# Mixture-of-experts stage of a decoder block: down weights in whole rows, shared PSUM accumulators, scatters in the next block

## The chip, the core and the metric

The kernel runs on one core of one Trainium2 chip; the other cores are idle. The metric is the device time of one execution in microseconds, taken as the median of several runs. One further execution was taken with the hardware profiler; all rows shown come from it.

## What is computed

The reference is one decoder layer for 512 tokens of width 2048, all in float32: a shared RMSNorm with modulation, sparse attention beside gated linear attention, an output projection, then a mixture of experts and a final RMSNorm. The change is in the mixture of experts alone, which has 32 experts in 4 groups of 8. Each token picks its best group and two experts in it:

```
def expert_ffn(args):
    xb, e = args
    return (jax.nn.silu(xb @ w_gate[e]) * (xb @ w_up[e])) @ w_down[e]

y = lax.map(expert_ffn, (x_slots, blk_expert)).reshape(cap, D)
y = y * slot_w[:, None].astype(y.dtype)
y = jnp.zeros((N + 1, D), y.dtype).at[slot_tok].add(y)[:N]
```

`w_gate` and `w_up` are 2048 x 512 for each expert and `w_down` is 512 x 2048, 4 MiB each. So the stage reads 32 x 12 MiB = 402.7 MB of weights once. Its result, times a gate vector g2, is added to the residual stream x.

## The kernel before, in words

Everything up to the routing takes the first half of the time. It ends with `x1`, the residual stream (4 tiles of 128 tokens), with its normalized copy in two parts whose sum keeps float32 precision (`h2h`, `h2l`), and with each token's places and weights for the experts. Then the experts are sorted by their number of tokens, and the stage runs in **blocks** of 128 token slots (`Block`, L1160). The first block has experts 0 and 1 with 64 slots each. Eleven blocks follow (L1365 to L1367): eight with three experts (one of 64 slots and two of 32), and three with two experts of 64 slots, which come third, sixth and ninth of these eleven. So there are twelve blocks, and the last has three experts. A loop for experts with more tokens than slots comes behind and runs only if it is needed.

A block does the following, for the four chunks n of 512 input columns:

- `gather(n, i)` (L1171): two matmuls with the one-hot matrix G bring the rows of token tile i into the slots; after i = 3, ACT copies the sum out as `xe`.
- `turn(n)` (L1181): four transposes on PE and four ACT activations, which also apply the modulation, give `xt`.
- `gate_up(n, which)` (L1192): for each expert of the block one load of 1 MiB of gate (`which` 0) or up (`which` 1) weights, then the products into two PSUM accumulators `pgu`. The source of a load is 512 whole rows of the matrix, four consecutive ones to a partition, which makes 8192 consecutive bytes for each partition (`load_in`, L1142).

After the last chunk ACT and DVE form silu(gate) x up. `weights` (L1207) makes the transposed one-hot matrix `T` and the slot weights `ws`, and `turn_up` (L1218) transposes the activation to `aT`. Then come the down products, in four steps `down(hf, kk)` (L1226): hf is the half of the 2048 output columns, kk the half of the 512 inner rows. A step loads for each expert 256 rows by 1024 columns, 1 MiB, two pieces of 4096 bytes for each partition (`load_down`, L1153). Each half uses two PSUM accumulators `pd`; after its second step DVE, ACT and DVE again weigh each of the two chunks of 512 columns and split it in two parts `yh`, `yl` (L1241 to L1245). `scatter(n, i)` (L1248) multiplies them with `T` (two matmuls into `pss`) and DVE adds the product to token tile i of `x1` (L1253).

PSUM has eight banks, two each for the tags `pst`, `pgu`, `pd` and `pss` (L1106, `pB`). The weights go through a ring of seven tiles of 1 MiB, four of the pool `ring` and three of `lm` (`wtile`, L1125); all loads are issued by SP in the order of the program, and a load waits until PE has released the tile seven loads before it. PE's order is fixed by hand: `then` (L1258) chains each step behind the one before.

`run_block` (L1266) sets this order. Scatters of output chunks 0 and 1 lie in the block's own down stretch, those of chunks 2 and 3 are woven between the gathers of the next block's chunks 1 and 2:

```
for i in range(NT):
    then(blk.gather, n + 1, i)
    if left and i in (0, 2):
        then(prev.scatter, 2 + n, i // 2)
if left:
    then(prev.scatter, 2 + n, 2)
    then(prev.scatter, 2 + n, 3)
...
then(blk.turn, n + 1)
```

`begin_next` (L1369) makes the one-hot matrix of the next block on DVE and its weighted form on POOL. The last block cuts its last chunk in two (`cuts`, L1376).

## Time and profile before

| what | us |
|---|---|
| median of 3 runs | 2143.22 (2139.55 to 2144.33) |
| profiled execution | 2135.08 |
| its span, first to last instruction | 2133.4 |
| PE busy in it | 1934.6 (91%) |
| DVE busy | 947.4 (44%) |
| ACT busy | 677.0 (32%) |

The profile is of the one execution named. PE is the tensor engine's matmuls and PEld its weight loads, which overlap them; a busy PE is not PE at its peak, since matmuls are pipelined. The DMA share is the mean busy share of the 16 DMA engines, and PEclk the clock granted to PE as a share of 2.4 GHz. A row of the windows gives the stretch, its length, the busy us (and instructions) of PE, PEld, DVE, ACT and POOL, then PEclk, the DMA share and GB/s. A float32 product stands as two matmul rows. An arrow names who ended an idle time.

### The profile page before, as it was taken

Reading aid. Unit: us, or ns where it says so; the run is one execution under the profiler, and the core shown is the slowest. Engines: PE = TensorE matmul, PEld = TensorE weight load, DVE = VectorE, ACT = ScalarE, POOL = GpSimd, SP = SyncE. Lnnn points to the kernel's source line nnn. Section 1 sums busy time; section 2 is a strip of 40 time slices with the busy share of each in tenths; the row PEclk is TensorE's granted clock in tenths of the full one; section 3 lists DMA queues with packets and bytes.
Section 4 is the critical chain, followed back from the end, with each engine's and each line's share of the span. In section 5 each row is a group of like instructions: output and inputs, shape, how many; then the busy total and the mean of one; then the engine's idle time right before and its main releaser. Section 6 shows DMA issues by size and latency. Waiting matters only on the chain. (4 is left out here: it accounts for less than half of the span.)

```text
span 2133.4 us, 29142 instructions
## 1 busy us (share of the span) xinstructions
PE 1934.6 (91%) x11126; PEld 1129.4 (53%) x11126; DVE 947.4 (44%) x2098; ACT 677.0 (32%) x1443; POOL 57.5 (3%) x112
## 2 busy tenths in 40 slices
PE   6989999999999999999979888997889888998885
PEld 4646777777777787877734332442324323343322
DVE  4667876468764965576352121230212311221205
ACT  4433567466543443323342101111112111111112
POOL 0001000000000000100000000000000000000000
PEclk8999999999999999999989999999999999999998
DMA  8996735326463774676248999999999999999995
GB/s 289 315 296 168 207 107 130 88 63 182 122 183 95 219 207 133 222 268 220 99 186 334 413 403 405 397 401 406 413 394 376 419 404 415 397 390 408 394 414 184
DMA packets 241891, 595.42 MB, mean 279 GB/s; under 512 B 23154, under 2 KB 105272, under 8 KB 208724
## 3 DMA queue, kind: packets, MB, share of 16 engines
q1 hardware_dynamic: 227424, 583.05, 74.1%
q10 hardware_dynamic: 11764, 6.27, 1.1%
q0 software_dynamic: 2560, 4.20, 1.0%
q8 instruction: 89, 1.46, 0.3%
q14 instruction: 54, 0.44, 0.1%
HBM read 580.37 MB, written 7.86 MB: 276 GB/s over the span
## 5 line engine op out<-in xcount | busy, mean ns | idle before, releaser
L1199 PE MATMUL pgu<-raw,xt 128*32 128x512 f32 (+1 forms) x2544 | 404.4, 606 | 64.4 <-DMA raw<-in_w_expert_gate_dram 45.2
L1199 PEld LDWEIGHTS pgu<-raw,xt 128*32 128x32 f32 (+1 forms) x2544 | 110.2, 116 | 323.5 <-issue 199.3
L1234 PE MATMUL pd<-raw,aT 128*32 128x512 f32 (+1 forms) x1280 | 246.4, 598 | 31.8 <-DMA raw<-in_w_expert_down_dram 22.1
L360 PE MATMUL pj<-hthi,wlo 128*128 128x512 f32 (+1 forms) x624 | 250.6, 402 | 4.0 <-DVE wlo L355 3.9
L358 PE MATMUL pj<-hthi,whi 128*128 128x512 f32 (+1 forms) x624 | 251.4, 403 | 0.7 <-ACT a L403 0.7
L359 PE MATMUL pj<-htlo,whi 128*128 128x512 f32 (+1 forms) x624 | 249.6, 400 | 0.5 <-issue 0.5
L1253 DVE TENSOR_TENSOR x<-x,pss 128x512 f32<-128x512 f32 (+1 forms) x196 | 127.1, 674 | 257.8 <-PE pss L1252 257.6
L163 DVE SCALAR_TENSOR_TENSOR acc<-raw,csil,acc 128x512 f32<-128x512 f32 x296 | 222.1, 751 | 27.9 <-DMA raw<-in_w_ada_dram 23.5
L1234 PEld LDWEIGHTS pd<-raw,aT 128*32 128x32 f32 (+1 forms) x1280 | 69.8, 114 | 193.3 <-issue 104.0
L1178 ACT COPY xe<-pst 128x512 f32<-128x512 f32 x48 | 28.1, 585 | 391.8 <-PE pst L1175 391.8
L354 ACT CAST whi<-raw 128x512 fp32r<-128x512 f32 (+1 forms) x156 | 94.9, 614 | 177.0 <-PE pj L359 162.4
L355 DVE TENSOR_TENSOR wlo<-raw,whi 128x512 fp32r<-128x512 f32 (+1 forms) x156 | 105.4, 681 | 88.0 <-ACT whi L354 81.9
L360 PEld LDWEIGHTS pj<-hthi,wlo 128*128 128x128 f32 (+1 forms) x624 | 116.6, 187 | 29.9 <-DVE wlo L355 5.2
L358 PEld LDWEIGHTS pj<-hthi,whi 128*128 128x128 f32 (+1 forms) x624 | 116.7, 187 | 26.5 <-issue 3.6
L359 PEld LDWEIGHTS pj<-htlo,whi 128*128 128x128 f32 (+1 forms) x624 | 116.6, 187 | 26.0 <-issue 4.4
L1243 ACT CAST y<-y 128x512 fp32r<-128x512 f32 (+1 forms) x49 | 29.8, 609 | 295.0 <-DVE y L1241 291.6
L1241 DVE SCALAR_TENSOR_TENSOR y<-pd,ws,g2b 128x512 f32<-128x512 f32 (+1 forms) x49 | 36.1, 737 | 170.8 <-PE pd L1234 170.7
L1251 PE MATMUL pss<-y,T 128*128 128x512 f32 (+1 forms) x196 | 87.4, 446 | 14.7 <-DVE x L1253 14.2
L1188 ACT ACTIVATE xt<-pst,modp,w2p 128x128 f32<-128x128 f32 x192 | 73.5, 457 | 37.6 <-PE pst L1185 37.6
L1174 PE MATMUL pst<-h2h,G 128*128 128x512 f32 x192 | 80.9, 421 | 1.4 <-DVE G L1028 1.2
L606 ACT ACTIVATE s<-s,mx 128x128 f32<-128x128 f32 (+3 forms) x128 | 70.9, 556 | 18.5 <-DVE mx L604 17.9
L1252 PE MATMUL pss<-y,T 128*128 128x512 f32 (+1 forms) x196 | 76.6, 391 | 0.0
(479 smaller groups left out, 2668.8 us busy)
## 6 DMA issues: line engine op xcount, KB each, us to landing
raw<-in_w_expert_down_dram SPq DMA_DIRECT2D x128, 1024.0 KB, 11.8
raw<-in_w_expert_gate_dram SPq DMA_DIRECT2D x127, 1024.0 KB, 11.5
raw<-in_w_expert_up_dram SPq DMA_DIRECT2D x127, 1024.0 KB, 10.1
raw<-in_w_ada_dram SPq DMA_DIRECT2D x96, 1024.0 KB, 6.7
raw<-in_w_in_dram SPq DMA_DIRECT2D x38, 1024.0 KB, 6.1
raw<-in_w_out_dram SPq DMA_DIRECT2D x16, 1024.0 KB, 5.2
raw<-in_x_dram SPq DMA_DIRECT2D x8, 1024.0 KB, 6.2
rkv<-in_w_in_dram SPq DMA_DIRECT2D x4, 1024.0 KB, 9.1
```

What stands on the lines that cost most here:

```text
L163: nc.vector.scalar_tensor_tensor(acc, wt[:, k], csil[:, kt:kt + 1], acc, op0=OP.mult, op1=OP.add)
L354: nc.scalar.copy(hi[:, :, 0:n], src)
L355: nc.vector.tensor_sub(lo[:, :, 0:n], src, hi[:, :, 0:n].bitcast(F32))
L358: nc.tensor.matmul(ps[:n], hi[:, k, 0:n], hthi[kt // 4][:, kt % 4], start=(kt == 0), stop=False)
L359: nc.tensor.matmul(ps[:n], hi[:, k, 0:n], htlo[kt // 4][:, kt % 4], start=False, stop=False)
L360: nc.tensor.matmul(ps[:n], lo[:, k, 0:n], hthi[kt // 4][:, kt % 4], start=False, stop=(kt == KT - 1))
L1174: nc.tensor.matmul(self.pg, self.G[:, i], h2h[n][:, i], start=(i == 0), stop=False)
L1199: ins = nc.tensor.matmul(self.gu[which][s0:s0 + u], self.xt[n][:, k, s0:s0 + u], wts[x][k], start=(n == 0 and k == 0), stop=(n == 3 and k ...
L1234: ins = nc.tensor.matmul(self.pd[c][s0:s0 + u], self.aT[:, 2 * kk + k, s0:s0 + u], wts[x][:, k, 512 * c:512 * c + 512], start=(kk == 0 and ...
L1251: nc.tensor.matmul(ps, self.T[:, 128 * i:128 * i + 128], yh, start=True, stop=False)
L1252: ins = nc.tensor.matmul(ps, self.T[:, 128 * i:128 * i + 128], yl, start=False, stop=True)
L1253: nc.vector.tensor_add(x1[:, i, c0:c0 + cn], x1[:, i, c0:c0 + cn], ps)
```

## The change

Down weights are loaded in another cut: step k of four takes for each expert rows 128k to 128k + 127 of `w_down` whole, so each partition gets one row of 8192 consecutive bytes (`load_rows`); the number and size of loads stay. A step multiplies into all four output chunks, so four accumulators are open at once (`down_rows`); gate, up and down share four PSUM banks under one tag `acc` in place of two times two. The weighing becomes a method `weigh(n)`: chunks 0 and 1 are weighed after the down products, chunks 2 and 3 in the next block's chunks 0 and 1. All four scatters move into the next block, one output chunk in each of its four input chunks, between `turn` and the up products; the gathers of a chunk now stand ahead of its gate products, except in the first block. The last block keeps the old down steps and its two own scatters.

```diff
--- before.py
+++ after.py
@@ -1106,7 +1106,7 @@
     psB = LM.enter_context(tc.tile_pool(name="psB", bufs=2, space=PSUM))
 
     def pB(tag):
-        return psB.tile([128, 512], F32, name=tag, tag=tag)
+        return psB.tile([128, 512], F32, name=tag, tag=tag, bufs=4 if tag == "acc" else 2)
 
     g2b = []
 
@@ -1149,6 +1149,12 @@
             return t
         nc.sync.dma_start(t, src)
         return [t[:, k] for k in range(4)]
+
+    def load_rows(e, k):
+
+        t = wtile().rearrange("p k f -> p (k f)")
+        nc.sync.dma_start(t, one(wd_, e)[:, 128 * k:128 * k + 128].rearrange("o p c -> p (o c)"))
+        return t
 
     def load_down(e, kk, hf):
 
@@ -1191,7 +1197,7 @@
 
         def gate_up(self, n, which):
             if n == 0 and which == 0:
-                self.gu = pB("pgu"), pB("pgu")
+                self.gu = pB("acc"), pB("acc")
             wts = [load_in((wg_, wu_)[which], e, n) for e, _, _ in self.experts]
             u = self.unit
             for k in range(4):
@@ -1223,27 +1229,44 @@
             nc.scalar.copy(self.aT, ps.rearrange("p (j s) -> p j s", j=4))
             return ins
 
+        def down_rows(self, k):
+
+            if k == 0:
+                self.pd = [pB("acc") for _ in range(4)]
+            wts = [load_rows(e, k) for e, _, _ in self.experts]
+            u = self.unit
+            for n in range(4):
+                for x, s0 in self.parts:
+                    ins = nc.tensor.matmul(self.pd[n][s0:s0 + u], self.aT[:, k, s0:s0 + u],
+                                           wts[x][:, 512 * n:512 * n + 512], start=(k == 0), stop=(k == 3))
+            return ins
+
         def down(self, hf, kk):
+
             if kk == 0:
-                self.pd = pB("pd"), pB("pd")
+                if hf == 0:
+                    self.pd = [None] * 4
+                self.pd[2 * hf:2 * hf + 2] = pB("acc"), pB("acc")
             wts = [load_down(e, kk, hf) for e, _, _ in self.experts]
             u = self.unit
             for c in range(2):
                 for k in range(2):
                     for x, s0 in self.parts:
-                        ins = nc.tensor.matmul(self.pd[c][s0:s0 + u], self.aT[:, 2 * kk + k, s0:s0 + u],
+                        ins = nc.tensor.matmul(self.pd[2 * hf + c][s0:s0 + u], self.aT[:, 2 * kk + k, s0:s0 + u],
                                                wts[x][:, k, 512 * c:512 * c + 512], start=(kk == 0 and k == 0),
                                                stop=(kk == 1 and k == 1))
                 if kk == 1:
-                    n = 2 * hf + c
-                    for c0, cn in self.cuts if n == 3 else ((0, 512),):
-                        ys, yh, yl = (mp.tile([128, 512], dt, name="y", tag="yz", bufs=5)[:, 0:cn] for dt in (F32, F32R, F32R))
-                        nc.vector.scalar_tensor_tensor(ys, self.pd[c][:, c0:c0 + cn], self.ws, g2b[n][:, c0:c0 + cn],
-                                                       op0=OP.mult, op1=OP.mult)
-                        nc.scalar.copy(yh, ys)
-                        nc.vector.tensor_sub(yl, ys, yh.bitcast(F32))
-                        self.y.setdefault(n, []).append((512 * n + c0, cn, yh, yl))
+                    self.weigh(2 * hf + c)
             return ins
+
+        def weigh(self, n):
+            for c0, cn in self.cuts if n == 3 else ((0, 512),):
+                ys, yh, yl = (mp.tile([128, 512], dt, name="y", tag="yz", bufs=5)[:, 0:cn] for dt in (F32, F32R, F32R))
+                nc.vector.scalar_tensor_tensor(ys, self.pd[n][:, c0:c0 + cn], self.ws, g2b[n][:, c0:c0 + cn],
+                                               op0=OP.mult, op1=OP.mult)
+                nc.scalar.copy(yh, ys)
+                nc.vector.tensor_sub(yl, ys, yh.bitcast(F32))
+                self.y.setdefault(n, []).append((512 * n + c0, cn, yh, yl))
 
         def scatter(self, n, i):
             for c0, cn, yh, yl in self.y[n]:
@@ -1266,21 +1289,28 @@
     def run_block(blk, prev, begin_next):
 
 
+        last = len(blk.cuts) > 1
+
+        def gather(n):
+            before_gather(blk, n)
+            for i in range(NT):
+                then(blk.gather, n, i)
+
         for n in range(4):
+            if n < 3 and blk is not first:
+                gather(n + 1)
             then(blk.gate_up, n, 0)
             if n < 3:
-                before_gather(blk, n + 1)
-                left = prev is not None and n < 2
+                if blk is first:
+                    gather(n + 1)
+                then(blk.turn, n + 1)
+            if prev is not None:
                 for i in range(NT):
-                    then(blk.gather, n + 1, i)
-                    if left and i in (0, 2):
-                        then(prev.scatter, 2 + n, i // 2)
-                if left:
-                    then(prev.scatter, 2 + n, 2)
-                    then(prev.scatter, 2 + n, 3)
-                elif n == 2:
-                    then(blk.weights)
-                then(blk.turn, n + 1)
+                    then(prev.scatter, n, i)
+                if n < 2:
+                    prev.weigh(n + 2)
+            if n == 3:
+                then(blk.weights)
             then(blk.gate_up, n, 1)
         nxt = begin_next()
         if not g2b:
@@ -1291,14 +1321,20 @@
         then(blk.turn_up)
         if nxt is not None:
             then(nxt.turn, 0)
-        then(blk.down, 0, 0)
-        then(blk.down, 0, 1)
-        then(blk.down, 1, 0)
-        for i in range(NT):
-            then(blk.scatter, 0, i)
-        then(blk.down, 1, 1)
-        for i in range(NT):
-            then(blk.scatter, 1, i)
+        if last:
+            then(blk.down, 0, 0)
+            then(blk.down, 0, 1)
+            then(blk.down, 1, 0)
+            for i in range(NT):
+                then(blk.scatter, 0, i)
+            then(blk.down, 1, 1)
+            for i in range(NT):
+                then(blk.scatter, 1, i)
+        else:
+            for k in range(4):
+                then(blk.down_rows, k)
+            blk.weigh(0)
+            blk.weigh(1)
         return nxt
 
 
@@ -1464,7 +1500,7 @@
     rsqrt_small(ssf, ssf, (128, NT), 1.0 / D)
     nfb = []
     for n in range(4):
-        ps = pB(("pst", "pd")[n % 2])
+        ps = pB(("pst", "acc")[n % 2])
         for j in range(4):
             nc.tensor.transpose(ps[:, 128 * j:128 * j + 128],
                                 colv[:, 48 + 4 * n + j:49 + 4 * n + j].to_broadcast([128, 128]), ident)
```

## Rows read from the trace of the kernel before

**Rows 1.** Page, section 2: GB/s in 40 slices, DMA packets.
```profile
GB/s 289 315 296 168 207 107 130 88 63 182 122 183 95 219 207 133 222 268 220 99 186 334 413 403 405 397 401 406 413 394 376 419 404 415 397 390 408 394 414 184
DMA packets 241891, 595.42 MB, mean 279 GB/s; under 512 B 23154, under 2 KB 105272, under 8 KB 208724
```

**Rows 2.** Windows, gate and up stretches: busy us by engine, PEclk, DMA share, GB/s.
```profile
1170.00:1210.00 40.00, 35.27 (x230) 14.91 (x222) 6.62 (x10) 6.84 (x17) 1.29 (x2) 1.00 1.01 418
1262.00:1302.00 40.00, 35.29 (x223) 14.99 (x222) 7.54 (x11) 6.96 (x17) 1.22 (x1) 1.00 1.01 417
1418.00:1458.00 40.00, 36.14 (x244) 15.32 (x236) 7.23 (x12) 6.84 (x17) 1.29 (x2) 1.00 1.01 417
1512.00:1552.00 40.00, 34.64 (x221) 14.58 (x221) 6.68 (x11) 6.84 (x17) 1.20 (x1) 1.00 1.01 413
1672.00:1712.00 40.00, 35.24 (x226) 14.98 (x222) 6.62 (x10) 6.84 (x17) 1.28 (x2) 1.00 1.01 418
1764.00:1804.00 40.00, 35.37 (x222) 14.95 (x222) 6.69 (x11) 6.84 (x17) 1.20 (x1) 1.00 1.01 414
1920.00:1960.00 40.00, 36.79 (x252) 15.70 (x244) 7.39 (x12) 7.16 (x18) 1.20 (x2) 1.00 1.00 408
```

**Rows 3.** Windows, down stretches of the same blocks.
```profile
1225.00:1245.00 20.00, 16.76 (x92) 3.91 (x90) 2.80 (x4) 2.72 (x6) 0.00 (x0) 1.00 1.02 381
1318.00:1338.00 20.00, 16.41 (x98) 4.87 (x98) 2.80 (x4) 2.99 (x7) 0.00 (x0) 1.00 1.02 390
1475.00:1495.00 20.00, 16.49 (x97) 4.84 (x96) 2.79 (x4) 2.90 (x7) 0.00 (x0) 1.00 1.02 389
1568.00:1588.00 20.00, 15.88 (x85) 4.07 (x88) 2.80 (x4) 3.56 (x8) 0.00 (x0) 1.00 1.01 382
1727.00:1747.00 20.00, 16.36 (x97) 5.03 (x98) 2.80 (x4) 3.23 (x7) 0.00 (x0) 1.00 1.02 387
1819.00:1839.00 20.00, 16.38 (x97) 4.97 (x99) 2.80 (x4) 3.81 (x8) 0.00 (x0) 1.00 1.02 392
1978.00:1998.00 20.00, 15.91 (x89) 4.62 (x89) 2.80 (x4) 3.50 (x8) 0.00 (x0) 1.00 1.01 373
```

**Rows 4.** Groups by line, 1150 to 2110 us: busy us, mean ns, idle before.
```profile
L1234 PE MATMUL pd<-raw,aT 128*32 128x512 f32 (+1 forms) x1268 | 243.8, 598 | 31.8 <-DMA raw<-in_w_expert_down_dram 22.1 <-DVE y L1241 8.9 <-ACT aT L1223 0.7
...
L1241 DVE SCALAR_TENSOR_TENSOR y<-pd,ws,g2b 128x512 f32<-128x512 f32 (+1 forms) x49 | 36.1, 737 | 170.8 <-PE pd L1234 170.7
```

**Rows 5.** Waits of SP's DMA queue, 1150 to 2110 us: total us, times, longest.
```profile
SPq L1150 <- PE pgu L1199: 353.4, 79, 7.3
```

**Rows 6.** Windows in two-expert blocks: gate and up, then down.
```profile
1348.00:1380.00 32.00, 30.93 (x139) 14.80 (x138) 10.29 (x18) 5.38 (x12) 0.25 (x1) 1.00 0.97 393
...
1895.00:1906.00 11.00, 9.94 (x44) 4.43 (x43) 2.11 (x3) 3.61 (x8) 0.00 (x0) 1.00 1.03 410
```

**Rows 7.** Timeline of PE, around the first scatter of a two-expert block's down stretch.
```profile
1655.36 3.69 PE L1234 MATMUL pd<-raw,aT 128*64 128x512 f32 x14 [0.97 <-DVE y L1241]
1658.98 0.50 PE L1251 MATMUL pss<-y,T 128*128 128x512 f32 x1
...
1661.75 3.71 PE L1234 MATMUL pd<-raw,aT 128*64 128x512 f32 x16
```

**Rows 8.** Timeline of PE: gathers with a woven scatter, gathers alone, and a turn.
```profile
1354.09 0.50 PE L1174 MATMUL pst<-h2h,G 128*128 128x512 f32 x1
...
1358.53 7.09 PE L1199 MATMUL pgu<-raw,xt 128*64 128x512 f32 x32
...
1390.94 0.51 PE L1174 MATMUL pst<-h2h,G 128*128 128x512 f32 x1
...
1392.91 0.60 PE L1221 MATMUL pst<-ident,sg__11453 128*128 128x128 f32 x4
1393.80 0.66 PE L1185 MATMUL pst<-ident,xe 128*128 128x128 f32 x4 [0.29 <-ACT xe L1178]
```

**Rows 9.** Window in the last block's down stretch.
```profile
2071.00:2091.00 20.00, 16.47 (x93) 3.85 (x88) 2.80 (x4) 1.24 (x2) 0.00 (x0) 1.00 1.01 387
```

## The prediction

> **What bounds the kernel now.** I read first the page's strip of 40 slices with the DMA packet line, because it shows where the time lies [rows 1]. The reader is to see that from slice 23 on, that is over the expert stage and some 45% of the span of 2133.4 us, the DMA engines move about 400 GB/s without a pause. Then I cut windows out of that stage, in pairs from the same block of three experts: a stretch in which only gate and up weights arrive [rows 2], and one in which only down weights arrive [rows 3]. The DMA share is 1.00 to 1.02 in both, and PE is busy for only about 35 of 40 us and 16 of 20 us, so the transfers set the pace. But the rate is not the same. The seven gate and up stretches give 418, 417, 417, 413, 418, 414 and 408 GB/s, mean 415.0. The seven down stretches give 381, 390, 389, 382, 387, 392 and 373, mean 384.9. Both kinds of load are 1 MiB each on the same queue; what differs is the row: 8192 bytes to a partition for gate and up, two pieces of 4096 bytes for down. The packet line has 208,724 of 241,891 packets under 8 KB, and the 128 down loads account for 128 x 256 = 32,768 of these.
>
> Next the groups by line say what PE's down matmuls wait for: of 31.8 us idle, 22.1 us for the down weights and 8.9 us for the evacuation of the accumulators (first line of [rows 4]). The queue's own waits say that SP in turn waits for PE to release a weight buffer, 353.4 us in 79 waits at the gate and up loads alone [rows 5]. With seven buffers, this is the ring breathing: as long as a load is still outstanding when SP is let go, the wait costs nothing, and the DMA share of 1.0 says that this is so in three-expert blocks. In two-expert blocks it is only nearly so: the gate and up stretch at 1348 us has a DMA share of 0.97, 393 GB/s, and PE busy for 30.93 of 32 us [rows 6]. There PE is the bound and the buffers run full.
>
> **The change, part by part.** There are twelve blocks: the first with two experts, eight with three, three with two. All but the last, which has three, load their down weights in the new way: 29 experts x 4 = 116 loads.
>
> Row length. A load of 1,048,576 bytes takes 2.724 us at 384.9 GB/s and 2.527 us at 415.0. If a down load then goes as a gate load does, the gain is 0.198 us each, 116 x 0.198 = 22.9 us, on the path, since the DMA engines are the bound around these loads. Bounds: the closest pair of windows (392 and 408) gives 0.105 us a load, 12.2 us; the farthest (373 and 418) gives 0.302, 35.1 us. I take the mean, because the down loads come to look exactly like the gate loads: one run of 8192 bytes to a partition, 1 MiB in one piece of memory. A smaller gain is possible too. The down stretch of a two-expert block reached 410 GB/s with 4096-byte rows [rows 6]; were that the true rate of such rows, 410 against 415 gives 0.031 us a load and 3.6 us in all.
>
> The Trainium skill, "DMA: Bandwidth & Descriptors", Specifications, puts the line-rate threshold at 512 bytes, and its section "Why small descriptors are slow (HBM only)" charges some 3 cycles per packet beside a beat per 32 bytes. By this, 4096 bytes cost 131 and half of 8192 bytes 129.5, an estimate of 1.1% or 3.6 us in all. The windows disagree: they show 7% between the two row lengths.
>
> Shared accumulators. The wait of 8.9 us goes, as no second pair has to be claimed in the middle of the down products. It costs and gives nothing: right behind it PE waits for down weights anyway. In its place gate and up of the next block need the two banks of output columns 0 and 1. The last down step takes PE 3.7 us [rows 7] and finishes column 0 first, and eight gather matmuls now lie ahead of the first gate product, 2.0 us [rows 8]; one DVE evacuation of 0.74 us fits (second line of [rows 4]). Without the gather it would cost about 1 us a block, 11 us.
>
> Scatters moved. Per block two scatters (8 matmuls and 4 DVE adds each) and two weighings (two DVE operations and one ACT copy each) leave the down stretch for the next block's gate and up stretch; no DMA is issued in them. SP issues the same loads in the same order, 1 MiB each, 12 or 8 to a block's down stretch; POOL's product for the next block stays behind the same step. A scatter alone takes PE 2.8 us, from 1658.98 to 1661.75 us [rows 7]. In three-expert blocks a step's three loads take 7.6 us and its products under 4 us, so a turn and a scatter, about 3.7 us, just fit between gate and up of one chunk. Cost nothing; without that cover, some tenths of a microsecond per step.
>
> In two-expert blocks there is no such cover, since PE is the bound in the gate and up stretch. It gets one scatter more than now, 2.8 us, and the two that were woven between gathers now stand alone: woven with a turn they took 4.4 us (1354.09 to 1358.53) against 2.0 (1390.94 to 1392.91) + 0.7 + 2.8 = 5.5 us apart [rows 7, 8]. That is 2.8 + 2 x 1.1 = 5.0 us later per block at the end of that stretch, and its down stretch loses the scatter and the wait of 0.97 us, 3.7 us. Bounds: nothing, if the seven buffers bridge it and the shorter down stretch gives it back, and 5.0 us in each of the three blocks, 15 us, if they don't. The row at 393 GB/s shows them already at their limit (5% of 32 us, 1.7 us lost); I take about as much again, 1.5 us a block, 4.5 us.
>
> Sum: 22.9 - 4.5 = 18.4 us less. The profiled execution took 2135.08 us, 1.7 us more than its span; it would come to 2116.7 us. The three runs shown have a median of 2143.22 us, 8.1 us above that execution. I predict for such runs: 2143.2 - 18.4 = **2124.8 us**.
>
> **The rivals.**
> (a) Row length doesn't matter; the thin down stretches come from how SP is let go in them, and only 3.6 us are won and 4.5 us lost: 2144.1 us, no change. For it: one down stretch at 410 GB/s. Against it: SP is let go in the same way, by steps of three loads, in the gate and up stretches, and these keep 408 to 418. By the threshold of the Trainium skill (the page and section named above) it would come out this way too.
> (b) The two-expert blocks pay in full: 22.9 - 15 = 7.9 us less, 2135.3 us. For it: PE's 30.93 of 32 us. Against it: the down stretch behind gives most of it back.
> (c) Slower: the scatters filled PE's waits, and without them PE's clock falls to 1.2 GHz (0.5) in the down stretches. Its products there, 4 x 3.7 = 14.8 us a block, would take 29.6. In the three two-expert blocks that exceeds the 20.2 us of 8 loads by 9.4 us each, 28 us; in the seven others of three experts every release of a buffer comes 3.7 us late, and paying this once each makes 26 us. Together 54 - 18.4 = 36 us more, 2179 us; it decides from the point where a third of the down stretches run at half clock. Against it: the last block's down products from 2071 to 2091 us already run with no scatter among them and show a granted clock of 1.00 [rows 9].
> That the rows are not really joined I hold for excluded but for a rest: gate and up loads of the same form do give 8192-byte packets.
>
> **How the numbers follow.** Forecast 0.65 (2108 to 2136 us: 35.1 won and nothing lost, or 12.2 won and 4.5 lost); (a) 0.14; (b) 0.10; (c) 0.07; a gain beyond the bounds 0.04. Anything within 0.2% (4.3 us) is about what a measurement of this kernel cannot tell from no change. Faster by more than that: the forecast, the far gain and nearly all of (b), 0.78. Within it: (a) and a rest of (b), 0.14. Slower: (c) and a little of (a), 0.08. For 8 in 10 the range runs from 2110 to 2138 us: it takes in the forecast but for its thinnest edge, and (b), and leaves out (a), (c) and the far gain.
>
> **What would show it.** The packets should fall by 116 x 128 = 14,848, all from those under 8 KB. Windows of down loads should read 410 GB/s or more, at a DMA share of 1.0; if they stay near 385, the main step is wrong. PE's wait for the evacuation should nearly vanish, with its wait for weights as long as now. Two-expert gate and up stretches should show a DMA rate a little under 393; far under it, (b) holds. A granted clock of 0.5 in down stretches would be (c). A profiled span above 2128 us (2138 less the 8.1 and 1.7 us above) would make the prediction wrong.

## The result, and the profile after

The changed kernel is faster. Its median is 2114.26 us (4 runs, 2113.23 to 2118.59), against 2141.39 us for the kernel before, run beside it on the same chip (4 runs, 2139.21 to 2144.33): a ratio of 0.9883 with a 95% interval of 0.9871 to 0.9894. That is 25 us less by the ratio (1.17% of 2141.39); the two medians by themselves give 0.9873 or 27.1 us, within the interval. 2124.8 us were forecast, with a range from 2110 to 2138, so the direction and the mechanism held, and the gain came out larger than the sum of 18.4 us. The profiled execution took 2114.3 us, with a span of 2112.6 us against 2133.4 us before.

The page's strip of slices and packet line of the changed kernel answer to [rows 1]:

```profile
GB/s 304 310 294 161 204 121 112 109 56 159 132 179 108 192 220 160 188 262 259 104 140 300 420 419 420 418 388 419 419 420 402 406 419 419 419 385 419 419 411 179
DMA packets 227043, 595.42 MB, mean 282 GB/s; under 512 B 23154, under 2 KB 105272, under 8 KB 179028
```

There are 14,848 packets fewer than before, exactly 116 x 128. Of those under 8 KB there are 29,696 fewer, which is 116 x 256: each of the 116 loads turned 256 short packets into 128 long ones. The bytes are the same. In the expert stage the strip now reads 418 to 420 in most slices, where before it wandered between 376 and 419; three places stay low (388, then 402 and 406, then 385), and these are the three two-expert blocks.

Windows of the changed kernel, first two of the seven gate and up stretches of three-expert blocks, which answer to [rows 2] (busy us and instructions of PE, PEld, DVE, ACT and POOL, then granted clock, DMA share, GB/s); then four down stretches, which answer to [rows 3] and, the last of them, to [rows 9]; then the two-expert block of [rows 6], first in the window of before and then in pieces of 10 us:

```profile
1170.00:1210.00 40.00, 34.85 (x212) 12.86 (x210) 10.28 (x16) 6.40 (x15) 1.20 (x2) 1.00 1.01 419
1920.00:1960.00 40.00, 35.25 (x217) 14.79 (x217) 9.61 (x15) 6.33 (x16) 1.21 (x2) 1.00 1.01 419
1228.00:1248.00 20.00, 20.00 (x102) 6.48 (x94) 0.00 (x0) 0.00 (x0) 0.00 (x0) 1.00 1.01 420
1563.00:1583.00 20.00, 20.00 (x101) 6.49 (x94) 0.00 (x0) 0.00 (x0) 0.00 (x0) 1.00 1.01 418
1962.00:1982.00 20.00, 20.00 (x106) 6.55 (x101) 0.00 (x0) 0.00 (x0) 0.00 (x0) 1.00 1.01 419
2052.00:2072.00 20.00, 15.30 (x80) 3.93 (x73) 2.80 (x4) 1.24 (x2) 0.00 (x0) 1.00 1.01 378
1350.00:1382.00 32.00, 31.14 (x136) 13.04 (x138) 9.90 (x17) 5.95 (x14) 1.21 (x2) 1.00 0.98 396
1370.00:1380.00 10.00, 9.68 (x46) 3.87 (x44) 3.02 (x6) 1.72 (x5) 1.21 (x2) 1.00 1.00 400
1380.00:1390.00 10.00, 9.69 (x44) 3.68 (x40) 3.17 (x5) 1.29 (x3) 0.00 (x0) 1.00 0.93 372
1390.00:1400.00 10.00, 9.70 (x44) 5.02 (x44) 0.69 (x1) 2.58 (x6) 0.00 (x0) 1.00 0.85 315
1400.00:1410.00 10.00, 10.00 (x43) 3.94 (x40) 1.47 (x3) 0.62 (x1) 0.00 (x0) 1.00 1.01 421
```

The reader is to see three things. The down stretches now run at the rate of gate and up, 418 to 420 GB/s, where they had 373 to 392; the last block, which still loads half rows, stays at 378 in the very same execution. The granted clock in the down stretches is 1.00. And in the two-expert block the rate falls for about 30 us, down to 315 GB/s at a DMA share of 0.85, while PE is busy for 9.7 of 10 us: there the buffers run full and PE is the bound (from 1350 to 1400 us PE waits for no weights at all).

What PE's products wait for, as groups by line over the whole execution, and as waits (us in total, times, longest) from 1150 to 2090 us; L1240 is the new down product, L1255 the old one of the last block:

```profile
L1205 PE MATMUL acc<-raw,xt 128*32 128x512 f32 (+1 forms) x2544 | 407.9, 608 | 40.5 <-DMA raw<-in_w_expert_gate_dram 39.9
...
L1240 PE MATMUL acc<-raw,aT 128*32 128x512 f32 (+1 forms) x1152 | 246.7, 596 | 0.0
```

```profile
PE acc L1205 <- DMA raw<-in_w_expert_gate_dram: 39.9, 36, 1.8
PE pss L1274 <- DVE x L1276: 15.9, 50, 0.5
PE acc L1255 <- DMA raw<-in_w_expert_down_dram: 4.7, 4, 1.7
```

The wait for the evacuation, 8.9 us in [rows 4], is gone, and so, against the prediction, are the 22.1 us of waiting for down weights: the new down products show no idle time at all. That comes with the row steps (the four steps of `down_rows`) and not with the faster loads: half rows in the same steps (e6 below) leave 2.5 us of this wait, whole rows in the old half steps of `down` (e7) 25.6 us. Nor does it make PE the bound of these stretches. e7 moves the same bytes at 422 GB/s with PE busy for only 6.83 of 8 us and takes the same time, and e6 shows PE busy for 8.00 of 8 us while its loads crawl at 334 GB/s.

Last, where in time the gain lies. Each block has one `turn_up`, so its transposes can serve as marks. The timelines of PE, the first and the last of these marks, of the kernel before and then of the changed kernel:

```profile
1145.39 0.60 PE L1221 MATMUL pst<-ident,sg__10063 128*128 128x128 f32 x4
...
2069.16 0.66 PE L1221 MATMUL pst<-ident,sg__15133 128*128 128x128 f32 x4 [0.85 <-DVE sg__15133 L1204]
```

```profile
1147.55 0.60 PE L1227 MATMUL pst<-ident,sg__10063 128*128 128x128 f32 x4
...
2048.21 0.66 PE L1227 MATMUL pst<-ident,sg__15133 128*128 128x128 f32 x4 [0.93 <-DVE sg__15133 L1210]
```

Between these marks lie the products with all 116 loads of the new form. The way takes 923.8 us before and 900.7 us after, 23.1 us less. The first block reaches its mark 2.2 us later. Its order up to there is nearly the same in both kernels, and from its first gate product to its mark it takes between 51.7 and 54.5 us in the traces of all versions, so these 2.2 us cannot be told from the difference between executions. The rest behind the last mark is as long as it was (64.2 and 64.4 us).

### The profile page after: what moved, and what is told of

Its sections match the earlier page's. It is cut to its first block, busy times and chain, and to the rows that moved or that the text cites. A ratio compares the mean times of both kernels' runs of the same rounds, so it can differ in the third digit from the quotient of the medians.

```text
span 2112.6 us, 29141 instructions
## 1 busy us (share of the span) xinstructions
PE 1965.5 (93%) x11126; PEld 1145.9 (54%) x11126; DVE 946.0 (45%) x2098; ACT 678.3 (32%) x1443; POOL 56.2 (3%) x112
## 4 chain that ended last, share of the span: by engine, by line
PE 37%; DMA 17%; DVE 4%; ACT 2%; issue 1%; POOL 0%; POOLq 0%; ACTq 0%; DVEq 0%
DMA raw<-in_w_expert_gate_dram 16%; PE acc L1205 12%; PE acc L1240 10%; PE pst L1180 1%; PE pss L1274 1%; PE pst L1181 1%; PE pj L890 1%; PE pj L892 1%; PE pj L891 1%; PE sc L890 1%; PE sc L891 1%; PE sc L892 1%; DVE x L1276 1%; PE pst L1191 1%; DVE h2l L997 1%; PE pss L1275 1%
## 5 line engine op out<-in xcount | busy, mean ns | idle before, releaser
L1205 PE MATMUL acc<-raw,xt 128*32 128x512 f32 (+1 forms) x2544 | 407.9, 608 | 40.5 <-DMA raw<-in_w_expert_gate_dram 39.9
L1205 PEld LDWEIGHTS acc<-raw,xt 128*32 128x32 f32 (+1 forms) x2544 | 115.2, 116 | 284.0 <-issue 183.2
L1240 PE MATMUL acc<-raw,aT 128*32 128x512 f32 (+1 forms) x1152 | 246.7, 596 | 0.0
L1240 PEld LDWEIGHTS acc<-raw,aT 128*32 128x32 f32 (+1 forms) x1152 | 80.5, 115 | 158.2 <-issue 145.0
L1265 DVE SCALAR_TENSOR_TENSOR y<-acc,ws,g2b 128x512 f32<-128x512 f32 (+1 forms) x49 | 36.2, 738 | 271.8 <-PE acc L1240 254.9
L1274 PE MATMUL pss<-y,T 128*128 128x512 f32 (+1 forms) x196 | 91.5, 467 | 16.3 <-DVE x L1276 15.9
L1275 PE MATMUL pss<-y,T 128*128 128x512 f32 (+1 forms) x196 | 76.9, 392 | 0.0
```

The lines of the kernel that those rows point to most:

```text
L1205: ins = nc.tensor.matmul(self.gu[which][s0:s0 + u], self.xt[n][:, k, s0:s0 + u], wts[x][k], start=(n == 0 and k == 0), stop=(n == 3 and k ...
L1240: ins = nc.tensor.matmul(self.pd[n][s0:s0 + u], self.aT[:, k, s0:s0 + u], wts[x][:, 512 * n:512 * n + 512], start=(k == 0), stop=(k == 3))
L1274: nc.tensor.matmul(ps, self.T[:, 128 * i:128 * i + 128], yh, start=True, stop=False)
L1275: ins = nc.tensor.matmul(ps, self.T[:, 128 * i:128 * i + 128], yl, start=False, stop=True)
```

## The experiments

Two theories were set against each other at first. The **row theory** is the forecast: the longer rows raise the rate, and everything else in the change is the price for them. The **order theory** says that the new order of release and the scatters' new place fill the thin stretches, and that the rows matter little. Later runs ask which property of a row matters. All ratios are to the kernel before, on the same chip.

| run | what it is | median us | ratio (95%) |
|---|---|---|---|
| changed kernel | | 2114.26 | 0.9883 (0.9871 to 0.9894) |
| e9_changed_again | the same once more | 2115.29 | 0.9888 (0.9870 to 0.9905) |
| e10_rows_all_old | before, whole rows alone | 2110.62 | 0.9871 (0.9854 to 0.9888) |
| e5_shared_acc | before, shared banks alone | 2140.17 | 1.0007 (0.9996 to 1.0018) |
| e2_halves_new_order | after, half rows | 2146.14 | 1.0040 (1.0026 to 1.0054) |
| e1_rows_old_order | after, scatters at their old places | 2127.61 | 0.9948 (0.9934 to 0.9961) |
| e6_halves_row_steps | after, half rows in the row steps | 2147.58 | 1.0041 (1.0024 to 1.0057) |
| e7_rows_half_steps | after, whole rows in half steps | 2114.39 | 0.9883 (0.9866 to 0.9900) |
| e3_pieces_4096 | after, 4096-byte pieces without gaps | 2120.42 | 0.9917 (0.9903 to 0.9930) |
| e11_every_second_row | after, 8192-byte rows with gaps | 2113.14 | 0.9884 (0.9867 to 0.9901) |
| e12_halves_adjacent | as e6, both halves in succession | 2147.07 | 1.0041 (1.0025 to 1.0056) |
| e4_late_scatter | two-expert blocks: last scatter later | 2117.30 | 0.9897 (0.9882 to 0.9912) |
| e8_woven_two | two-expert blocks: scatters woven | 2110.79 | 0.9862 (0.9844 to 0.9880) |

e10, e6, e7, e3, e11 and e12 leave the right result out: their products, equal in number and shape, take wrong parts of the weights. They price a form of load and are no kernels for use.

The marks of the section before also show where in the stage the time goes. Of the eleven stretches from one block's mark to the next, six lead into or out of one of the three two-expert blocks, four lie between three-expert blocks, and one leads out of the first block. Sums in us, each from one profiled execution:

| kernel | all eleven | the six at two-expert blocks | the four between three-expert blocks |
|---|---|---|---|
| before | 923.8 | 474.1 | 371.7 |
| changed | 900.7 | 464.3 | 359.8 |
| e9, changed again | 902.3 | 463.6 | 362.3 |
| e7, whole rows in half steps | 903.5 | 464.3 | 362.4 |
| e10, loads alone | 900.4 | 461.2 | 361.4 |
| e8, scatters woven | 895.5 | 459.2 | 359.7 |
| e1, scatters at their old places | 915.0 | 476.5 | 358.9 |
| e2, half rows in the new order | 931.6 | 480.4 | 372.7 |

### The parts alone

**The loads alone (e10).** The kernel before, with nothing but the source of its down loads changed; the last block keeps its own.

```diff
...
-            wts = [load_down(e, kk, hf) for e, _, _ in self.experts]
+            wts = [load_rows(e, 2 * hf + kk) if len(self.cuts) == 1 else load_down(e, kk, hf) for e, _, _ in self.experts]
```

> The kernel before with nothing changed but the loads: whole rows of 8192 bytes in place of the half rows, in the same steps by halves and with scatters and accumulators as before (the down products take wrong parts of the weights). If the load's gain (34 us, half rows against whole rows in the new order) and the order's loss (9 us, new against old order with half rows) simply add, ratio 0.983 to 0.986, below the changed kernel. If the new order only loses with half rows, or whole rows need the new order, 0.988 to 0.991 or more.

Measured: 0.9871, between the two expected ranges: the whole gain and perhaps a little more (27.6 us of 2137.95). A down stretch of this run, in a window of its trace:

```profile
1234.00:1242.00 8.00, 6.42 (x34) 1.44 (x32) 2.05 (x3) 1.15 (x2) 0.00 (x0) 1.00 1.02 422
```

The old steps, the old release and the old scatters, with whole rows, run at 422 GB/s. The kernel before has 342 in the same window:

```profile
1234.00:1242.00 8.00, 7.33 (x32) 1.41 (x29) 2.80 (x4) 1.24 (x2) 0.00 (x0) 1.00 1.01 342
```

So the source of the loads is enough for the gain. A product with a whole row reaches all four output chunks in one step, and the room for that is what the other edits provide.

**The shared banks alone (e5).** The kernel before with one tag of four banks in place of two of two.

```diff
-        return psB.tile([128, 512], F32, name=tag, tag=tag)
+        return psB.tile([128, 512], F32, name=tag, tag=tag, bufs=4 if tag == "acc" else 2)
...
-                self.gu = pB("pgu"), pB("pgu")
+                self.gu = pB("acc"), pB("acc")
```

> Only the third part of the change: the kernel before with gate, up and down sharing four PSUM banks, same loads and same order of steps. Both theories: no change, ratio 0.998 to 1.002; PE's waits for DVE's evacuation in the down products (8.9 us before) gone, its waits for weights longer by as much.

Measured: 1.0007, no change. The wait for the evacuation is gone, and the wait for weights has taken its place; PE's waits of this run, from 1150 to 2110 us:

```profile
PE acc L1255 <- DMA raw<-in_w_expert_down_dram: 31.2, 30, 2.3
```

31.2 us are the 22.1 and 8.9 us of [rows 4] together: a wait ahead of a later wait is worth nothing.

**Half rows in the new order (e2).** The changed kernel, with the old half steps in all blocks and the new places of scatters and weighings.

```diff
-            for k in range(4):
-                then(blk.down_rows, k)
-            blk.weigh(0)
-            blk.weigh(1)
+            blk.later = True
+            for hf in range(2):
+                for kk in range(2):
+                    then(blk.down, hf, kk)
...
```

> The changed kernel's order (all scatters in the next block, shared accumulators), but down weights in the old half rows of 4096 bytes in every block. If the row length is the cause, 2135 to 2146 us, as the kernel before, and down windows at 380 to 392 GB/s. If the order is the cause, 2114 to 2120 us and down windows over 410 GB/s.

Measured: 1.0040, slower than before by 8.6 us. The order without the rows loses, and by the marks it loses at the two-expert blocks: 6.3 us of 7.8. The window shows the old thin stretch:

```profile
1234.00:1242.00 8.00, 5.38 (x30) 1.43 (x31) 2.80 (x4) 1.24 (x2) 0.00 (x0) 1.00 1.00 327
```

**Rows without the moved scatters (e1).** The changed kernel with its row steps and four accumulators, but scatters 0 and 1 in the block's own down stretch, behind its last step (all four chunks are ready only there), and 2 and 3 woven into the next block as before. The gathers go back behind the gate products with them.

```diff
-            blk.weigh(0)
-            blk.weigh(1)
+            for n in range(4):
+                blk.weigh(n)
+                if n < 2:
+                    for i in range(NT):
+                        then(blk.scatter, n, i)
...
```

> The changed kernel's whole-row loads and four open accumulators, but the order of the kernel before: scatters 0 and 1 in the block's own down stretch (now behind all four down steps), 2 and 3 woven between the next block's gathers. If the row length is the cause (theory), nearly all of the gain of 27 us is here: 15 to 27 us under the kernel before, 2114 to 2126 us, and down windows at 415 to 419 GB/s. If the moved scatters are the cause (rival), within 6 us of the kernel before and down windows near 385 GB/s.

Measured: 0.9948, half the gain, between the two expected ranges; 0.65% or 14 us worse than the changed kernel. Windows of a down stretch and of a later stretch, and a new wait of PE, from 1150 to 2110 us:

```profile
1220.00:1250.00 30.00, 29.71 (x160) 10.38 (x153) 1.44 (x2) 2.94 (x7) 0.00 (x0) 0.99 1.02 420
1360.00:1370.00 10.00, 10.00 (x48) 4.97 (x44) 2.67 (x4) 2.09 (x5) 0.00 (x0) 1.00 0.86 338
```

```profile
PE pss L1275 <- DVE y L1268: 7.1, 11, 0.6
```

The loads run as fast as in the changed kernel (420), but the gain is lost after the down stretch: PE stands two scatters in a row there, with waits for the weighing, and frees no weight buffer meanwhile. By the marks the loss lies at the two-expert blocks, where PE is the bound: 12.2 us in their six stretches and 3.0 us behind the first block, and none between three-expert blocks. So with row steps the move of the scatters is needed there; it is no gain of its own (e2), it keeps the rows' gain.

### Order of release, or the rows themselves

Two runs cross the two properties: half rows loaded in the new row steps (e6), and whole rows loaded in the old half steps (e7), both with the scatters of the changed kernel.

```diff
-        t = wtile().rearrange("p k f -> p (k f)")
-        nc.sync.dma_start(t, one(wd_, e)[:, 128 * k:128 * k + 128].rearrange("o p c -> p (o c)"))
-        return t
+        t = wtile().rearrange("p (k c) f -> p k (c f)", k=2)
+        kk, hf = k % 2, k // 2
+        nc.sync.dma_start(t, one(wd_, e)[:, 256 * kk:256 * kk + 256, 1024 * hf:1024 * hf + 1024].rearrange(
+            "o (k p) c -> p (o k) c", p=128))
+        return t.rearrange("p k c -> p (k c)")
```

> The changed kernel with the half rows of the kernel before (two pieces of 4096 bytes to a partition, every second 4096 bytes of 256 rows), put in the place of the whole rows of each step; products, their order and the accumulators stay those of the changed kernel (so the down products take wrong parts of the weights). Theory: PE lets the buffers go one by one in a step over all four chunks, which keeps the transfers queued, and that made the slow patches vanish; then this is as the run with contiguous pieces of 4096 bytes, ratio to the kernel before 0.990 to 0.994 and down windows at 405 to 412 GB/s. Rival: the gaps between half rows in memory are slow to read; then ratio 0.999 to 1.005 and down windows at 370 to 392 GB/s.

```diff
...
-            wts = [load_down(e, kk, hf) for e, _, _ in self.experts]
+            wts = [load_rows(e, 2 * hf + kk).rearrange("p (k c) -> p k c", k=2) if self.later else load_down(e, kk, hf)
+                   for e, _, _ in self.experts]
...
```

> The other corner: the run with half rows in the new order, with its loads replaced by whole rows of 8192 bytes, and the products in the old steps by halves (two accumulators at a time, so wrong parts of the weights). Theory (order of release): SP is let go for a step's loads together again, so a part of the loss comes back: ratio to the kernel before 0.991 to 1.001, slow patches below 400 GB/s in or behind the down stretches. Rival (memory): as the changed kernel, 0.987 to 0.990, and 415 to 420 GB/s throughout the three-expert blocks.

Measured: 1.0041 for the half rows in row steps, 0.9883 for the whole rows in half steps. The time goes with the rows and not at all with the steps: e6 stands where e2 stands, e7 where the changed kernel stands. Three successive windows of one down stretch of e6, and then the middle one of e7:

```profile
1226.00:1234.00 8.00, 8.00 (x57) 2.51 (x56) 0.00 (x0) 1.51 (x4) 0.00 (x0) 1.00 1.02 403
1234.00:1242.00 8.00, 8.00 (x29) 1.93 (x28) 0.00 (x0) 0.00 (x0) 0.00 (x0) 1.00 0.99 334
1242.00:1250.00 8.00, 8.00 (x35) 2.28 (x35) 0.00 (x0) 0.00 (x0) 0.00 (x0) 1.00 1.03 417
```

```profile
1234.00:1242.00 8.00, 6.83 (x39) 1.67 (x34) 2.09 (x4) 1.24 (x2) 0.00 (x0) 1.00 1.02 422
```

The order theory falls. But e6 shows something new: half rows are not slow throughout. A step's three loads take about 7.6 us, so these windows stand roughly for one step each, the second to the fourth. Two of them have 403 and 417 GB/s, and one has 334, with the DMA share still at 0.99; the engines are occupied and move less. This is so in every block of three experts: windows of 8 us laid on the third step read 320 to 373 GB/s in the eight of e6 and 328 to 361 in the eight of the kernel before, whose second and fourth steps read 404 to 415 (the fourth without the last block).

### What it is about the half rows

A half row differs from a whole one in two ways: the piece is 4096 bytes long in place of 8192, and between two pieces lie 4096 bytes that are not read. Two runs separate them, both on the changed kernel.

**Short pieces without gaps (e3).** Each load reads the same 1 MiB in one piece of memory, but a partition takes two pieces of 4096 bytes from places 512 KiB apart.

```diff
-        t = wtile().rearrange("p k f -> p (k f)")
-        nc.sync.dma_start(t, one(wd_, e)[:, 128 * k:128 * k + 128].rearrange("o p c -> p (o c)"))
-        return t
+        t = wtile().rearrange("p (a c) f -> p a (c f)", a=2)
+        nc.sync.dma_start(t, one(wd_, e)[:, 128 * k:128 * k + 128].rearrange("o (a q) (h c) -> (q h) (o a) c", a=2, h=2))
+        return t.rearrange("p a c -> p (a c)")
```

> The changed kernel, each down load still one contiguous MiB of 128 whole rows and consumed in the same steps, but laid out so that each partition gets two pieces of 4096 bytes, 512 KiB apart (the down products then take wrong rows of the weights; their number and shape are the same). If the length of the piece is the cause, the gain is lost: 2133 to 2143 us, down windows 380 to 392 GB/s. If it is the gap of 4096 bytes between half rows in memory that was slow, or the order, it stays at 2112 to 2118 us with down windows near 419.

Measured: 0.9917, 0.34% or 7 us above the changed kernel and between the two expected ranges. Windows:

```profile
1226.00:1234.00 8.00, 8.00 (x51) 2.60 (x46) 0.00 (x0) 0.00 (x0) 0.00 (x0) 1.00 1.03 410
1234.00:1242.00 8.00, 8.00 (x35) 2.20 (x33) 0.00 (x0) 0.00 (x0) 0.00 (x0) 1.00 1.03 410
```

410 GB/s and steady, without the patch at 334. So the length alone is worth 2.2% of a load (410 against 419), a good fifth of the difference between e6 and the changed kernel (1.58%).

**Whole rows with gaps (e11).** Each load takes every second row of a block of 256.

```diff
-        nc.sync.dma_start(t, one(wd_, e)[:, 128 * k:128 * k + 128].rearrange("o p c -> p (o c)"))
+        nc.sync.dma_start(t, one(wd_, e)[:, 256 * (k // 2):256 * (k // 2) + 256].rearrange("o (p r) c -> p r (o c)", r=2)[:, k % 2])
```

> The changed kernel, each down load still 128 whole rows of 8192 bytes, but every second row of 256, so that memory is read with gaps of 8192 bytes (wrong rows for the products). If gaps between the pieces are what made half rows slow, whatever their length, ratio 0.993 to 1.002 and slow patches below 400 GB/s in the down stretches. If it takes pieces of 4096 bytes and gaps together, ratio 0.987 to 0.991 and 415 to 420 GB/s.

Measured: 0.9884, as the changed kernel; the window reads 418:

```profile
1234.00:1242.00 8.00, 8.00 (x37) 2.68 (x38) 0.00 (x0) 0.00 (x0) 0.00 (x0) 1.00 1.01 418
```

Gaps between whole rows cost nothing. The larger part, 1.24% or 26 us (e6 against e3), came only in the runs that have short pieces and gaps together. One more thing sets these apart from e3: a partition's two pieces lie 1 MiB apart in them and 512 KiB in e3. No run separates this distance from the gaps.

**The other half at once (e12).** As e6, but the two halves of a set of rows are read in successive steps, so that the third step reads other addresses than in e6.

```diff
-        kk, hf = k % 2, k // 2
+        kk, hf = k // 2, k % 2
```

> The run with half rows in row steps (ratio 1.004), with the order of a block's four steps changed: the second half of a set of 256 rows is loaded right after its first half, not after the first half of the other 256 rows. The slow loads were those of the third step, the second half of the first 256 rows. If the address makes them slow, the second step is now slow (and perhaps the fourth) and the ratio stays at 1.002 to 1.006. If it is the place in the stretch, the third step stays slow, same ratio. If the return to rows read some 15 us earlier is slow, the patches go, ratio 0.990 to 0.995.

Measured: 1.0041, as e6. The slow patch stays in its window; the window ahead of it, about the second step, which now reads what e6 reads in its slow third, has 393 GB/s:

```profile
1234.00:1242.00 8.00, 7.62 (x28) 1.94 (x28) 0.00 (x0) 0.00 (x0) 0.00 (x0) 1.00 0.99 341
```

The third window of the stretch, roughly its third step, is slow whichever half is read there. It is thus not the address of one half; why short pieces with gaps go slowly there and hardly elsewhere stays open.

### The two-expert blocks

The windows after show PE as the bound for some 30 us in each of these blocks. Against 419 GB/s the three thin windows lack (19 + 47 + 104) / 419 x 10 us = 4.1 us a block. Two runs try to win this back.

**Moving work within the block (e4).** The fourth scatter and `weights` go between the down steps 1 and 2.

```diff
...
+        late = prev is not None and len(blk.experts) == 2
...
+                if late and k == 1:
+                    for i in range(NT):
+                        then(prev.scatter, 3, i)
+                    then(blk.weights)
...
```

> The changed kernel, with the fourth scatter of the block before and the step that makes T and the slot weights moved, in the three blocks of two experts alone, from the gate and up stretch to between down steps 1 and 2. If PE's lag at the end of these gate and up stretches is what leaves the DMA engines idle there (DMA share 0.86 to 0.94 over some 30 us, about 4 us a block), 2 to 4 us a block come back: 2102 to 2108 us, and the windows around the turn of the activation read over 400 GB/s. If the idle time comes from something else (the order of the ring, the burst of releases), no change: 2112 to 2117 us.

Measured: 0.9897, no gain. Windows from 1390 us on, of this run:

```profile
1390.00:1400.00 10.00, 9.69 (x37) 3.88 (x36) 0.91 (x2) 1.15 (x4) 0.00 (x0) 1.00 1.00 415
1400.00:1410.00 10.00, 10.00 (x40) 4.09 (x40) 3.01 (x5) 1.03 (x3) 0.00 (x0) 1.00 0.98 362
1410.00:1420.00 10.00, 9.68 (x62) 4.31 (x64) 5.35 (x9) 3.51 (x8) 0.00 (x0) 1.00 0.97 383
```

The thin place has only moved 10 us on, where the changed kernel is back at 421.

**Weaving (e8).** In two-expert blocks the scatters alternate with the gathers, behind the gate products; the fourth alternates with the next block's first gather.

```diff
...
+            if two:
+                then(blk.gate_up, n, 0)
+                if n < 3:
+                    for i in range(NT):
+                        then(blk.gather, n + 1, i)
+                        then(prev.scatter, n, i)
+                    then(blk.turn, n + 1)
...
```

> The changed kernel, with the scatters of the three two-expert blocks woven between gathers (chunk n with the gather of n + 1, the fourth with the first gather of the next block), and T and the slot weights made after that. If it is PE's total work in a two-expert block that leaves the DMA engines idle (moving a scatter within the block had won nothing), the 0.3 us waits for DVE and the matmuls' gaps that weaving hides, some 0.8 us for each of 4 scatters, come back: 2 to 3 us a block, ratio to the kernel before 0.983 to 0.987 against 0.988 to 0.990 for the changed kernel. If not, 0.988 to 0.990.

Measured: 0.9862, the lowest median of a full version, 3.5 us under that of the changed kernel; but the intervals (0.9844 to 0.9880, and 0.9871 to 0.9894) overlap, so the times alone do not show the gain. The trace speaks for it: the way between the marks is 895.5 us against 900.7 and, in e9, 902.3, and 5.1 and 4.4 us of that lie in the six stretches at two-expert blocks, where the edit is (459.2 against 464.3 and 463.6). The marks, and two windows of it, beside 372 and 315 of the changed kernel:

```profile
1150.18 0.60 PE L1227 MATMUL pst<-ident,sg__10063 128*128 128x128 f32 x4
...
2045.65 0.65 PE L1227 MATMUL pst<-ident,sg__15133 128*128 128x128 f32 x4 [0.85 <-DVE sg__15133 L1210]
```

```profile
1380.00:1390.00 10.00, 10.00 (x48) 3.62 (x45) 0.69 (x1) 0.76 (x2) 0.00 (x0) 1.00 0.91 364
1390.00:1400.00 10.00, 9.71 (x48) 5.30 (x48) 3.45 (x5) 3.27 (x8) 0.00 (x0) 1.00 0.95 382
```

**The changed kernel once more (e9)** gave the scale on the chip of e10 to e12.

> The changed kernel once more, for a comparison on the same chip as the three others: ratio 0.987 to 0.990 to the kernel before.

Measured: 0.9888.

## Why the prediction was right, and where it was off

**What bounds the stage: right.** The DMA engines bound the three-expert blocks, and the down loads ran under the rate of gate and up. Raising their rate shortened the kernel; taking away a wait of PE (e5) did not.

**Row length: right in kind, and in size with some luck.** This is the term that carries the difference. It was put at 22.9 us, with bounds of 12.2 and 35.1. The loads alone gave 27.6 us by the ratio (e10, old order, interval 24 to 31), and in the profiled executions the way between the marks is 23.4 us shorter than before; the two figures differ by what single executions can lie off, as said under the base. Both ends of the sum were off. I let down loads rise to the 415.0 GB/s of the gate and up windows before, and they reach 419, which all seven windows of [rows 2] read after the change, too. And I let them start at 384.9, from windows of 20 us that lie around the slow third step; windows of 32 us over nearly the whole of the same seven down transfers read 386, 397, 396, 379, 395, 398 and 377, mean 390. From 390 to 419 a load goes from 2.689 to 2.503 us, 0.186 us where the sum had 0.198, and 116 loads gain 21.6 us. The two errors nearly cancel, and that is luck. In the new order the loads are worth more, 1.57% or 34 us (e2 against e7, which has the same steps), near the upper bound.

My wording of the cause was too simple. "What differs is the row" holds, but the length of the piece accounts only for some 7 us (e3), and the rest came only with gaps as well, most plainly in the third step. The window pairs could not tell this, since the only half rows in the trace had gaps.

The Trainium skill, "DMA: Bandwidth & Descriptors", "Why small descriptors are slow (HBM only)", gives a fixed cost of about 3 cycles per packet, of which I had worked out an estimate of 1.1% between the two lengths. Where the trace shows the length alone, the rates differ by 2.2%: the same direction and twice the size. The line-rate threshold of 512 bytes in the same page's Specifications would have made rival (a) come out; the runs decide against it, as 4096-byte pieces stay below 8192-byte ones both without gaps (410) and with them.

**Shared accumulators at nothing: right,** and shown alone (1.0007 in e5). The reason given also held: the wait for the weights takes its place, 31.2 us where there were 22.1 and 8.9.

**Scatters moved, 4.5 us lost: right in sign and place, unsettled in size.** With half rows the new order costs 8.6 us (e2). With whole rows the changed kernel (e9) and e10 differ by 0.9888 to 0.9871, 3.6 us, with intervals that overlap. The marks of e10:

```profile
1143.89 0.60 PE L1226 MATMUL pst<-ident,sg__10063 128*128 128x128 f32 x4
...
2044.25 0.65 PE L1226 MATMUL pst<-ident,sg__15133 128*128 128x128 f32 x4 [0.85 <-DVE sg__15133 L1209]
```

Between them e10 takes 900.4 us and the changed kernel 900.7. e10 is ahead by 3.7 us at the first mark, and 2.9 of these it has already at its first gate product (1090.13 against 1093.04 us), ahead of the changed steps; so these two traces put no loss on the order as a whole. At the two-expert blocks they do: the changed kernel and e9 take 2.4 to 3.1 us more there than e10, for the three blocks together, where I had 4.5 and bounds of nothing and 15. With half rows it was 6.3 us (e2 against the kernel before). PE is the bound in these blocks, and it was so before. Three windows of the kernel before, in the same place as the 400, 372 and 315 GB/s of after:

```profile
1370.00:1380.00 10.00, 9.71 (x46) 4.24 (x46) 1.11 (x4) 2.09 (x5) 0.25 (x1) 1.00 0.94 377
1380.00:1390.00 10.00, 10.00 (x50) 3.55 (x52) 0.65 (x2) 2.68 (x7) 1.10 (x2) 1.00 0.94 323
1390.00:1400.00 10.00, 9.71 (x48) 4.84 (x46) 0.69 (x1) 2.58 (x6) 0.00 (x0) 1.00 1.02 393
```

Their sum is 1093 against 1087: the thin place moved back by 10 us and grew no deeper. With whole rows in the old order it is nearly gone: e10 reads 392, 416 and 419 in these windows. So the new order takes back what the rows would have given there. What I missed is that the move can't be judged as a loss or gain by itself: with row steps it is needed, or 14 us go (e1).

**Rival (a), release by steps: refuted** by e6 and e7. **Rival (b), the two-expert blocks pay in full: refuted** by the result. **Rival (c), the clock falls: refuted;** the granted clock is 1.00 in the down windows, with no scatter among the products.

**What would show it.** Of the six marks, the packets, the down windows, the vanished evacuation wait, the clock and the span (2112.6 us) came as said. Two details did not. PE's wait for down weights was to stay as long as now, and fell from 22.1 us to none outside the last block; I had not seen that the row steps take it away, whatever the loads do (2.5 us in e6, 25.6 in e7). And the two-expert stretch was to read a little under 393 in its window and reads 396: its thin part lies behind the window's end, at 1380 to 1400 us.

**The base.** I took the profiled execution to lie 8.1 us under the median after the change too. It lies at the median there (2114.3 and 2114.26 us). So the profiled executions differ by 20.8 us, near the sum of 18.4, and the medians by 27.1. One execution can lie some microseconds off, and part of the miss in the predicted time is this and not a step of the argument.

## What to carry to other kernels

Where transfers bound a stage, compare the rate of its streams at a DMA share of 1.0: if one stream is slower at the same share, change the form of that source first, and try it alone in the old order, even with a wrong result, since one line showed the whole gain here. Then count the other edits as the price of that form, and look where they free buffers late: the scatters left at their place cost half the gain, nearly all of it at the blocks in which PE was already the bound. And lay the windows over the whole of a stream: mine caught the slow third step more than its share, and only a second error hid it.

## What was not expected of the hardware

Pieces of 4096 bytes with 4096-byte gaps do not lower the rate evenly. In e6 they run at 403 and 417 GB/s in the second and fourth window of a stretch; in the third they run at 327 to 342 in the four kernels that have such loads in this block (before, e2, e6, e12), at a DMA share of 0.99 to 1.01, whichever half of the rows is read there. All eight three-expert blocks show it: 328 to 361 GB/s before, 320 to 373 in e6, 325 to 368 in e12, in windows of 8 us on the third step. Pieces of 4096 bytes without gaps keep a steady 410, and 8192-byte rows reach 417 to 422, with gaps of 8192 bytes or without. The cause of the slow third step was not found.

The Trainium skill, "DMA: Bandwidth & Descriptors", "Where 436 GB/s comes from", has the memory side bind a load at some 358 GB/s, which it works out as a stack's 716 GB/s divided by two cores. The trace here shows 419 held through whole stretches of 40 us by one core with the others idle, so for one core alone the measurement decides; no run here has two cores loading.
